# Up projection by seven block products, weight sums in DRAM, out-projection in token halves

## The chip, the cores and the metric

One core of a Trainium2 chip runs the whole kernel. The metric is the device time of one execution in microseconds (us). On this core TensorE (PE) does the matrix products and reads its stationary operand by a weight load of its own (PEld); VectorE (DVE), ScalarE (ACT) and GpSimd (POOL) do the rest, and SyncE (SP) issues all DMAs.

## The reference, cut to what matters

One layer over 16 meta rows and 2048 input rows of width 1024. The kernel cuts the rows into four segments of 512; segment 0 carries the meta rows as well. The part that is changed is the gated MLP and what leads to it.

```python
h = h + mix @ w_out                      # out-projection, 1024 x 1024
z = rmsnorm(h, norm2_g)                  # "z2" in the kernel
u, v = jnp.split(z @ w_up, 2, axis=-1)   # w_up: 1024 x 5632, so D_FF = 2816 = 22 blocks of 128
u = causal_dwconv(u, conv_w, conv_b)     # width 3 along the rows
h = h + (jax.nn.silu(u) * v) @ w_down
```

Everything is float32. The kernel makes each product of two float32 matrices from three passes in the type fp32r: every operand is split into a high part and a low rest, and high x high, high x low and low x high are summed in PSUM. A product over K = 1024 for a 128 x 512 output is therefore 8 x 3 = 24 matmuls.

## The kernel before

`trunk_layer` loops over the four segments `s`. A segment has these stages, in program order: four head pairs of the recurrence (projections f and q, `decays`, `all_scores`, `chunks_out`); the pooling branch; the gates and `mix` (lines 597 to 611); the out-projection (lines 614 to 633); the product `values` for the next segment (lines 647 to 650); and the MLP (lines 654 to 709) in three groups of 8, 8 and 6 units, each followed by its down projection.

`weights()` (line 78) brings one 128 x 1024 block of weights: a DMA of 512 KB into a `raw` buffer (three of them), a cast on ACT for the high part (line 85), a subtraction on DVE for the low part (line 86), both into a `w` buffer (three of them). `proj` (line 101) multiplies such a block with columns of an activation; `rows_product` (line 126) multiplies rows of an activation with weight blocks, over all row chunks for each block, and calls a hook in `between` after each second k.

The out-projection makes h1 for all four chunks of 128 rows, in two halves of the columns (`dh`), 8 weight blocks in all; each block serves 24 matmuls. Between them, as hooks, stand the steps of `norm1(s + 1)`: the first norm of the next segment's rows, transposed and split into `z1`. Then DVE works out the second norm (`inv_rms`), scales the rows (`zt`, line 642), PE transposes them, and ACT and DVE split them into `z2` (`transposed`, line 172). In segments 0 to 2 `to_z2` is a hook inside `values(s + 1)`, which has 96 matmuls on z1; in segment 3 nothing stands beside it. z1 and z2 have buffers of their own.

One unit `j` of the MLP (lines 656 to 678): the u block (24 matmuls over 512 columns; in segment 0 two times 24 over 258 and 256), a copy to SBUF, the convolution on ACT and DVE, a sigmoid; then the v block (24 matmuls over 512 columns), its product with the activated u, and a split into `act`. Two weight blocks a unit.

The order on each engine is made by the framework's scheduler from priorities (program order) and estimated ready times; each engine then runs its own list in that order, and a wait at the head of a list holds what stands behind it. A buffer tag has a fixed number of slots; a new tile waits until a slot's last reader is done.

Of the kernel before, what the change touches and what calls it, by code (L numbers as in the profile page):

```python
# [44 lines left out]
def trunk_layer(ctx: ExitStack, tc: tile.TileContext, x, meta, wts, cst, gf, wpool, out):  # L45
# [6 lines left out]
    xpl = ctx.enter_context(tc.tile_pool(name="xpl", bufs=6))  # L52
# [3 lines left out]
    ps = ctx.enter_context(tc.tile_pool(name="ps", bufs=MM, space=bass.MemoryType.PSUM))  # L56

    V, A, G, T = nc.vector, nc.scalar, nc.gpsimd, nc.tensor

# [3 lines left out]
    for i, (o, n) in enumerate(zip(offs0, sizes0)):  # L63
        t = xpl.tile([P, D], F32, name="xt", tag="xh")
        nc.sync.dma_start(out=t[:n], in_=meta if n < P else x[o - META:o - META + P])
        xt0.append(t)
# [10 lines left out]

    def weights(lo=None):

        i = nxt[0]  # L80
        nxt[0] += 1
        raw = wpl.tile([P, 1024], F32, name="raw", bufs=RAW)
        nc.sync.dma_start(out=raw, in_=wts[i])
        w = wpl.tile([P, 2, 1024], F32R, name="w")
        A.copy(out=w[:, 0, :], in_=raw)  # L85
        (lo or V).tensor_tensor(out=w[:, 1, :], in0=raw, in1=w[:, 0, :].bitcast(F32), op=ALU.subtract)  # L86
        return w
# [38 lines left out]
    def rows_product(src, chunks, nk, consume, between=(), lo=None):  # L126

        banks = [ps.tile([P, 512], F32, name="rp", tag="hg", bufs=HG) if i < HG else
# [43 lines left out]
    def transposed(rows, sizes, offs, dst, gbase):  # L172

        banks = [[i for i in range(len(rows)) if offs[i] + sizes[i] <= 512],
                 [i for i in range(len(rows)) if offs[i] + sizes[i] > 512]]
        for k in range(KB):
            for idx in banks:
                if not idx:
                    continue
# [9 lines left out]
    def norm1_chunk(src, m, off, dst):  # L189
        t = xpl.tile([P, D], F32, name="xt", tag="xh")  # L190
# [19 lines left out]
    def norm1_first(xt, sizes, offs):  # L210

        dst = [blk.tile([P, 2, WMAX], F32R, name="z1") for _ in range(KB)]
# [15 lines left out]
        transposed(xt, sizes, offs, dst, C_G1)  # L228
        return dst

    def norm1(s):
# [3 lines left out]
        def one(c):  # L235
            if c == 0:
                dst.extend(blk.tile([P, 2, WMAX], F32R, name="z1") for _ in range(KB))
# [23 lines left out]
    def decays(f, N):  # L261

        nb = N // BASE
        scr = spl.tile([P, 10, 2 * WMAX // BASE], F32, name="scr", bufs=1)
        tt = spl.tile([P, 2, 2 * WMAX // BASE], F32, name="tt")
        f8 = f.rearrange("p (n j) -> p n j", j=BASE)
        r = [scr[:, i, :nb] for i in range(10)]
# [199 lines left out]
    for i in range(2):  # L467
# [16 lines left out]

    for s in range(nseg):
        nxt[0] = 0
# [9 lines left out]
        for p in range(PAIRS):  # L496
# [18 lines left out]
            main = (m0, NCH, P, W, at[p % 2], bt[p % 2])  # L515
# [98 lines left out]
        sizes2 = ([2] if s == 0 else []) + [P] * NCH  # L614
        offs2 = ([0] if s == 0 else []) + [e0 + c * P for c in range(NCH)]
        h1 = []
        for o, n in zip(offs2, sizes2):
# [3 lines left out]
            else:  # L621
                t = xpl.tile([P, D], F32, name="h1", tag="xh")
                nc.sync.dma_start(out=t, in_=x[s * SEG + o - e0:s * SEG + o - e0 + P])
            h1.append(t)
        chunks, z1n = norm1(s + 1) if s + 1 < nseg else ([], None)
        ss = new_sums(s == 0)
        for dh in range(2):
            def add_h(ci, bank):
                n = sizes2[ci]
                v = h1[ci][:n, dh * 512:(dh + 1) * 512]  # L630
                V.tensor_tensor(out=v, in0=v, in1=bank[:n, :], op=ALU.add)
                square_sums(ss[:n, dh, ci:ci + 1], v, n)
            rows_product(mix, list(zip(offs2, sizes2)), KB, add_h, chunks)


        z2 = [blk.tile([P, 2, WMAX], F32R, name="z2", tag="zo") for _ in range(KB)]
        rs = inv_rms(ss, len(h1))
        rows = []
        for i, n in enumerate(sizes2):
            zt = blk.tile([P, 2, WMAX], F32, name="zt", tag="am")  # L640
            zt = zt.rearrange("p a b -> p (a b)")[:, :D]
            V.tensor_scalar(out=zt[:n], in0=h1[i][:n], scalar1=rs[:n, i:i + 1], scalar2=None, op0=ALU.mult)
            rows.append(zt)
        to_z2 = lambda: transposed(rows, sizes2, offs2, z2, C_G2)


        if s + 1 < nseg:
            z1, vt = z1n, values(s + 1, z1n, between=[to_z2 if i == V_HOOK else (lambda: None) for i in range(V_HOOK + 1)])
        else:
            to_z2()  # L650
        nxt[0] = V_AT + KB // 2


        for (j0, nj) in GROUPS:
            act = [blk.tile([P, 2, WMAX], F32R, name="act", tag="am") for _ in range(nj)]
            for j in range(j0, j0 + nj):
# [124 lines left out]
```

## Time and profile before

| | us |
|---|---|
| median of 3 runs | 3143.08 (3140.93 to 3143.42) |
| the profiled execution, its own time | 3141.98 |
| its span, first to last instruction | 3140.2 |
| PE busy | 3080.5 (98%) |
| DVE busy | 1721.6 (55%) |
| ACT busy | 1136.8 (36%) |
| DMA | 294.86 MB, mean 94 GB/s |
| mean granted TensorE clock | 0.996 |

The profiled execution lies 1.1 us under the median and 1.8 us above its own span. PE's ends are modelled in this profile, so a busy share of a stage says that PE had work without a gap, and the time of one matmul is read from a stretch divided by the matmuls in it.

### The profile page before, as it was taken

To read this page: it belongs to the slowest core of one execution; us is meant where nothing else is said; L and a number is where in the kernel's file an instruction comes from. 1 tells how busy PE (TensorE), PEld (TensorE's weight loads), DVE (VectorE), ACT (ScalarE), POOL (GpSimd) and SP (SyncE) were. 2 spreads that over 40 slices of the span, in tenths; PEclk is the share of its full clock that TensorE was granted. 3 is DMA by queue.
4 is the path that set the end of the run, shared out by engine and by line. 5 is a ranking of instruction groups with operands and counts; after the bars stand their busy time and mean duration, and the time that the engine had idled before them with its cause. 6 is when DMAs were issued, how large, how long until landed. Compare 5 with 4: busy or idle time off the path is not lost.

```text
span 3140.2 us, 45714 instructions
## 1 busy us (share of the span) xinstructions
PE 3080.5 (98%) x19052; PEld 2552.0 (81%) x19052; DVE 1721.6 (55%) x2944; ACT 1136.8 (36%) x1765; POOL 48.9 (2%) x181
## 2 busy tenths in 40 slices
PE   7999999999999999999999999999999999999998
PEld 6899978898877788888877778888887778878887
DVE  5775364454487536544457744554456773354545
ACT  4333244232343325423333433433333432242323
POOL 1000000000000000000000000000000000000000
PEclk9999999999999999999999999999999999999999
DMA  4212232332331223223342133332333122223322
GB/s 153 62 62 81 88 108 88 94 95 93 99 125 62 88 94 114 94 94 94 95 153 69 55 99 105 100 98 94 94 101 128 55 81 94 94 81 94 94 94 88
DMA packets 81747, 294.86 MB, mean 94 GB/s; under 512 B 9074, under 2 KB 9202, under 8 KB 81540
## 3 DMA queue, kind: packets, MB, share of 16 engines
q1 hardware_dynamic: 81540, 291.95, 29.0%
q8 instruction: 149, 2.44, 0.3%
q14 instruction: 58, 0.48, 0.0%
HBM read 283.52 MB, written 8.39 MB: 93 GB/s over the span
## 4 chain that ended last, share of the span: by engine, by line
PE 92%; DVE 6%; ACT 1%; issue 0%; DMA 0%; SPq 0%; DVEq 0%; ACTq 0%
PE pt L108 61%; PE rp L137 24%; PE sp L300 1%; PE up L375 1%; DVE q L259 1%; DVE scr L259 1%; PE sp L312 1%; PE tp L185 1%; DVE k L259 1%; DVE q L513 1%; DVE w L86 1%; PE op L389 1%; PE ktp L366 0%; PE op L394 0%; PE pp L527 0%
## 5 line engine op out<-in xcount | busy, mean ns | idle before, releaser
L108 PE MATMUL pt<-z,w 128*128 128x512 f32 (+3 forms) x9552 | 1939.0, 362 | 0.0
L108 PEld LDWEIGHTS pt<-z,w 128*128 128x128 f32 x9552 | 1596.3, 189 | 296.9 <-issue 10.7
L86 DVE TENSOR_TENSOR w<-raw,w 128x1024 fp32r<-128x1024 f32 x500 | 612.3, 1225 | 1073.1 <-ACT w L85 1069.6
L85 ACT CAST w<-raw 128x1024 fp32r<-128x1024 f32 x504 | 528.3, 1048 | 745.8 <-PE rp L137 358.4
L137 PE MATMUL rp<-w,act 128*128 128x512 f32 x2040 | 474.1, 394 | 0.0
L137 PEld LDWEIGHTS rp<-w,act 128*128 128x128 f32 x2040 | 383.8, 188 | 88.5
L137 PE MATMUL rp<-w,mix 128*128 128x512 f32 (+1 forms) x816 | 192.7, 395 | 0.0
L662 ACT COPY ub<-pt 128x512 f32<-128x512 f32 (+1 forms) x110 | 55.3, 503 | 355.0 <-PE pt L108 355.0
L137 PEld LDWEIGHTS rp<-w,mix 128*128 128x128 f32 (+1 forms) x816 | 147.8, 182 | 39.1 <-issue 2.6
L669 DVE SCALAR_TENSOR_TENSOR cv<-ub,cs,cv 128x512 f32<-128x512 f32 x176 | 131.9, 749 | 3.1
L604 ACT ACTIVATE sg<-pt 128x512 f32<-128x512 f32 (+1 forms) x80 | 41.1, 513 | 239.1 <-PE pt L108 239.1
L672 ACT ACTIVATE sg<-cv 128x512 f32<-128x512 f32 x88 | 55.6, 632 | 178.5 <-DVE cv L669 178.5
L137 PE MATMUL rp<-w,z 128*128 128x512 f32 (+1 forms) x408 | 102.2, 402 | 0.0
L108 PE MATMUL pt<-oa,w 128*128 128x512 f32 (+2 forms) x480 | 95.1, 350 | 0.0
L108 PE MATMUL pt<-ob,w 128*128 128x512 f32 (+2 forms) x480 | 95.0, 350 | 0.0
L673 DVE TENSOR_TENSOR cv<-cv,sg 128x512 f32<-128x512 f32 x88 | 61.0, 693 | 61.5 <-ACT sg L672 61.5
L137 PEld LDWEIGHTS rp<-w,z 128*128 128x128 f32 (+1 forms) x408 | 74.0, 184 | 18.3 <-issue 0.4
L108 PEld LDWEIGHTS pt<-oa,w 128*128 128x128 f32 x480 | 77.9, 189 | 12.5
L108 PEld LDWEIGHTS pt<-ob,w 128*128 128x128 f32 x480 | 77.9, 189 | 12.5
L704 DVE TENSOR_TENSOR h<-h,rp 128x512 f32<-128x512 f32 x96 | 66.0, 688 | 29.1 <-PE rp L137 26.8
L609 DVE TENSOR_TENSOR sg<-sg,pt 128x512 f32<-128x512 f32 (+1 forms) x80 | 46.5, 582 | 62.7 <-PE pt L108 62.6
L95 ACT ACTIVATE z<-tp,cs 128x128 fp32r<-128x128 f32 (+3 forms) x152 | 61.0, 438 | 29.9 <-PE tp L185 12.8
(161 smaller groups left out, 1900.9 us busy)
## 6 DMA issues: line engine op xcount, KB each, us to landing
raw<-in_wts_dram SPq DMA_DIRECT2D x504, 512.0 KB, 3.6
xt<-in_x_dram SPq DMA_DIRECT2D x16, 512.0 KB, 4.5
h<-in_x_dram SPq DMA_DIRECT2D x16, 512.0 KB, 4.6
out_dram<-h SPq DMA_DIRECT2D x12, 512.0 KB, 3.0
gfb<-in_gf_dram SPq DMA_DIRECT2D x8, 256.0 KB, 4.3
out_dram<-h SPq DMA_DIRECT2D x8, 256.0 KB, 2.0
wp<-in_wpool_dram SPq DMA_DIRECT2D x1, 256.0 KB
cs<-in_cst_dram SPq DMA_DIRECT2D x1, 68.0 KB, 5.8
```

The source lines that it names most:

```text
L85: A.copy(out=w[:, 0, :], in_=raw)
L86: (lo or V).tensor_tensor(out=w[:, 1, :], in0=raw, in1=w[:, 0, :].bitcast(F32), op=ALU.subtract)
L95: A.activation(out=dst[0], in_=src, func=AF.Copy, scale=scale)
L108: T.matmul(pt[:, :n], lhsT=w[:, wi, (kof + k) * P:(kof + k + 1) * P], rhs=src[k][:, xi, c0 + o:c0 + o + n], start=(k == 0 and i == 0), sto ...
L137: T.matmul(banks[ci][:n, :], lhsT=src[k][:, xi, o:o + n], rhs=w[:, wi, (k % 2) * 512:(k % 2 + 1) * 512], start=(k == 0 and i == 0), stop=( ...
L259: mul = lambda o, a, b: V.tensor_tensor(out=o, in0=a, in1=b, op=ALU.mult)
L609: V.tensor_tensor(out=gates[i][:, o:o + n], in0=gates[i][:, o:o + n], in1=pt[:, :n], op=ALU.mult)
L662: A.copy(out=ub[:, 2 - e0 + o:2 - e0 + o + n], in_=pt[:, :n])
L669: V.scalar_tensor_tensor(out=cv, in0=ub[:, t_:t_ + SEG], scalar=col(C_CW + t_ * NF, j), in1=cv, op0=ALU.mult, op1=ALU.add)
L672: A.activation(out=sg, in_=cv, func=AF.Sigmoid)
L673: V.tensor_tensor(out=cv, in0=cv, in1=sg, op=ALU.mult)
L704: V.tensor_tensor(out=v, in0=v, in1=bank, op=ALU.add)
```

## The change

In segments 1 to 3 a unit's two blocks of the up projection are taken as one product: the activation side is two halves of the rows (256 columns each) by two halves of K (512 each), the weight side the four 512-deep blocks A11, A12 (u) and A21, A22 (v). A seven-product scheme replaces the eight block products. Each of the seven is 4 x 3 = 12 matmuls over 256 columns (`seventh`). Partial results in the PSUM banks X and Y are copied out by ACT four times a unit and put together by two DVE additions.

- The sums of weights (S1 to S4) are made on DVE in segment 0 (`weight_sums`, four additions of 512 columns a unit) and written to DRAM, `s_d`, with the split A11 and A12, `a_d`: four DMAs of 512 KB a unit. Segments 1 to 3 read per unit two `a_d` halves without splitting, two `s_d` blocks that are split again, and half a block of `wts` (A22). In units 0 to 2 A11 and A12 come from `wts` and are split.
- The activation side has seven slots: two direct quarters, a third quarter, four sums. `to_z2` makes them, once for the first half of the rows, once for the second.
- z1 and z2 share one tag of buffers (`z_plain`, four slots). `norm1(s + 1)` moves from the out-projection into the last down projection of the segment, and `values(s)` to the start of segment s.
- The out-projection runs once for each half of the rows, so that each weight block is brought twice (16 blocks a segment), and a block serves 12 matmuls.
- x and h rows get two tags (four and two slots), the recurrence's `scr` is taken from the second of them, and `at` and `bt` have one buffer instead of two.

The core of the diff:

```diff
+    def seventh(dst, w, xslot, start):
+        for kp in range(KP):
+            for i, (wi, xi) in enumerate(PASS):
+                T.matmul(dst, lhsT=w[:, wi, kp * P:(kp + 1) * P], rhs=z2[kp][:, xi, xslot],
+                         start=(start and kp == 0 and i == 0), stop=(kp == KP - 1 and i == 2),
+                         skip_group_check=True)
+    def q_open(j, iu):
+        if j < OPEN:
+            w = split_weights(wts[iu])[0]
+            a11, a12 = w[:, :, :512], w[:, :, 512:]
+        else:
+            a11, a12 = (blk.tile([P, 2, WMAX], F32R, name="wa", tag="zo")[:, :, :512] for _ in range(2))
+            for i, a in enumerate((a11, a12)):
+                nc.sync.dma_start(out=a.bitcast(F32), in_=a_d[j][i])
...
+        seventh(X[:, HT:], a11, 0, True)
+        seventh(Y[:, :HT], a12, 1, True)
+        A.copy(out=sx[:, :HT], in_=X[:, HT:])
+    def q_rest(j, ig, X, Y, sx, a):
+        w = split_weights(s_d[j][0])[0]
+        seventh(X[:, HT:], w[:, :, :512], 5, False)
+        seventh(Y[:, HT:], w[:, :, 512:], 3, True)
+        A.copy(out=sx[:, HT:], in_=X[:, HT:])
+        w = split_weights(s_d[j][1])[0]
+        seventh(X[:, HT:], w[:, :, :512], 4, False)
+        sy = vpl.tile([P, 512], F32, name="sy", tag="vt")
+        A.copy(out=sy[:, HT:], in_=Y[:, HT:])
+        seventh(Y[:, HT:], w[:, :, 512:], 2, False)
+        A.copy(out=sy[:, :HT], in_=X[:, HT:])
+        ub = new_ub(j)
+        V.tensor_tensor(out=ub[:, 2:2 + SEG], in0=Y, in1=sx, op=ALU.add)
...
+        w = split_weights(wts[ig, :, 512:], 512)[0]
+        seventh(X[:, :HT], w[:, :, :512], 6, True)
+        V.tensor_tensor(out=sy, in0=X, in1=sy, op=ALU.add)
+        gated(cv, sy, a)
+    def weight_sums(j, ru, rg, w):
+        a11, a12, a21, a22 = ru[:, :512], ru[:, 512:], rg[:, :512], rg[:, 512:]
...
+        V.tensor_tensor(out=s1, in0=a21, in1=a22, op=ALU.add)
+        V.tensor_tensor(out=s3, in0=a21, in1=a11, op=ALU.subtract)
+        V.tensor_tensor(out=s2, in0=s1, in1=a11, op=ALU.subtract)
+        V.tensor_tensor(out=s4, in0=a12, in1=s2, op=ALU.subtract)
+        for i in range(2):
+            nc.sync.dma_start(out=s_d[j][i], in_=t[i])
+            nc.sync.dma_start(out=a_d[j][i], in_=w[:, :, i * 512:(i + 1) * 512].bitcast(F32))
```

In `to_z2(half)` of segments 1 to 3, for each of four `kp`, behind four transposes:

```diff
+                for u in range(2):
+                    A.activation(out=a[:, 2 * u + half], in_=tp[:, u * HT:(u + 1) * HT], func=AF.Copy,
+                                 scale=col(C_G2, kp + u * KP))
+                if not half:
+                    split((z[:, 0, 0:2], z[:, 1, 0:2]), a[:, 0:3:2])
+                    continue
+                V.tensor_tensor(out=b[:, 0:2], in0=a[:, 1:2].broadcast_to([P, 2, HT]), in1=a[:, 0:4:3], op=ALU.subtract)
+                V.tensor_tensor(out=b[:, 2], in0=a[:, 3], in1=b[:, 0], op=ALU.subtract)
+                V.tensor_tensor(out=b[:, 3], in0=a[:, 2], in1=b[:, 2], op=ALU.subtract)
+                split((z[:, 0, 3:7], z[:, 1, 3:7]), b)
+                split((z[:, 0, 2], z[:, 1, 2]), a[:, 3])
```

The order in the first group of segments 1 to 3 (`OPEN` is 3):

```diff
+                    if j == 0:
+                        for i in range(OPEN):
+                            opened[i] = q_open(i, at_u(i))
+                            if i == OPEN - 2:
+                                to_z2(1)
+                    if j >= OPEN:
+                        opened[j] = q_open(j, at_u(j))
+                    q_rest(j, at_u(j) + 1, *opened.pop(j), act[j - j0])
```

A unit j of segment 0:

```diff
+                    cv = conv(j, ub)
+                    wg, rg = split_weights(wts[at_u(j) + 1])
+                    part(pg, 0, wg, e0, SEG)
+                    gated(cv, pg, act[j - j0])
+                    weight_sums(j, ru, rg, w)
```

## Rows read from the trace of the kernel before

**Rows 1.** Page, part 1: busy us, share of the span, instructions.

```profile
PE 3080.5 (98%) x19052; PEld 2552.0 (81%) x19052; DVE 1721.6 (55%) x2944; ACT 1136.8 (36%) x1765; POOL 48.9 (2%) x181
```

**Rows 2.** Page, part 4: the chain that ended last, by engine.

```profile
PE 92%; DVE 6%; ACT 1%; issue 0%; DMA 0%; SPq 0%; DVEq 0%; ACTq 0%
```

**Rows 3.** Windows: length, PE, PEld, DVE, ACT, POOL busy; clock, DMA share, GB/s.

```profile
1226.00:1255.50 29.50, 29.50 (x145) 24.25 (x144) 17.89 (x33) 13.59 (x24) 0.00 (x0) 1.00 0.30 90
...
2751.20:2763.70 12.50, 6.84 (x33) 6.29 (x34) 10.35 (x25) 6.52 (x13) 0.00 (x0) 0.73 0.15 43
```

**Rows 4.** Windows of line L108 alone: length, PE busy (matmuls), PEld, clock, DMA.

```profile
258.93:397.74 138.81, 138.81 (x1152) 138.60 (x1152) 1.00 0.30 92
...
1047.87:1181.19 133.32, 133.32 (x576) 108.01 (x576) 1.00 0.30 95
1255.46:1344.22 88.76, 88.76 (x384) 71.76 (x383) 1.00 0.30 94
```

**Rows 5.** Groups by form, PE: count, busy us, mean ns of one.

```profile
L108 PE MATMUL pt<-z,w 128*128 128x512 f32 x6576 | 1568.3, 396 | 0.0
...
L108 PE MATMUL pt<-z,w 128*128 128x256 f32 x1008 | 129.5, 284 | 0.0
```

**Rows 6.** Groups by form, ACT.

```profile
L85 ACT CAST w<-raw 128x1024 fp32r<-128x1024 f32 x504 | 528.3, 1048 | 745.8 <-PE rp L137 358.4 <-PE pt L108 273.4 <-DVE h L704 72.5
...
L92 ACT CAST act<-cv 128x512 fp32r<-128x512 f32 x88 | 54.5, 619 | 0.2 <-DVE cv L676 0.2
L662 ACT COPY ub<-pt 128x512 f32<-128x512 f32 x66 | 38.9, 589 | 268.9 <-PE pt L108 268.9
...
L662 ACT COPY ub<-pt 128x256 f32<-128x256 f32 x22 | 8.2, 372 | 54.4 <-PE pt L108 54.4
...
L95 ACT ACTIVATE ob<-pp,cs 128x256 fp32r<-128x256 f32 x4 | 1.9, 474 | 0.0
```

**Rows 7.** Groups by form, DVE.

```profile
L86 DVE TENSOR_TENSOR w<-raw,w 128x1024 fp32r<-128x1024 f32 x500 | 612.3, 1225 | 1073.1 <-ACT w L85 1069.6
...
L93 DVE TENSOR_TENSOR act<-cv,act 128x512 fp32r<-128x512 f32 x88 | 60.2, 685 | 0.0
...
L259 DVE TENSOR_TENSOR q<-q,tt 128x256 f32<-128x256 f32 x24 | 10.1, 423 | 2.0 <-PE sp L312 1.3
```

**Rows 8.** Windows of all engines in five stages, columns as in rows 3.

```profile
1181.20:1225.60 44.40, 44.40 (x208) 36.09 (x208) 30.06 (x89) 25.36 (x61) 0.00 (x0) 1.00 0.41 131
1255.46:1344.22 88.76, 88.76 (x386) 72.10 (x385) 45.33 (x54) 35.64 (x48) 2.44 (x16) 1.00 0.30 94
1588.46:1621.78 33.32, 33.32 (x146) 27.09 (x145) 13.61 (x16) 10.73 (x19) 0.00 (x0) 1.00 0.34 113
2.00:10.00 8.00, 0.00 (x0) 0.00 (x0) 4.81 (x21) 4.89 (x11) 1.68 (x4) 1.00 0.98 365
484.69:576.41 91.72, 91.72 (x578) 82.84 (x577) 45.52 (x54) 36.94 (x57) 1.48 (x8) 1.00 0.30 93
```

**Rows 9.** Timeline (start, us, instruction): transposes in segment 1; segment 3's gap.

```profile
1240.45 1.91 PE L185 MATMUL tp<-ident,zt 128*128 128x128 f32 x16
...
2749.14 2.77 DVE L631 TENSOR_TENSOR h<-h,rp 128x512 f32<-128x512 f32 x4 [1.15 <-PE rp L137]
...
2756.86 6.80 PE L185 MATMUL tp<-ident,zt 128*128 128x128 f32 x32 [5.67 <-DVE zt L642]
```

**Rows 10.** Windows in and after that gap, columns as in rows 3.

```profile
2757.00:2760.00 3.00, 3.00 (x14) 2.43 (x15) 1.71 (x4) 0.73 (x2) 0.00 (x0) 0.50 0.00 0
...
2763.40:2767.00 3.60, 3.60 (x19) 2.94 (x18) 1.99 (x3) 1.12 (x2) 0.00 (x0) 1.00 0.00 0
```

**Rows 11.** Timeline of one unit's end in segment 1, DVE.

```profile
1267.69 1.23 DVE L86 TENSOR_TENSOR w<-raw,w 128x1024 fp32r<-128x1024 f32 x1 [0.20 <-ACT w L85]
1268.83 0.69 DVE L93 TENSOR_TENSOR act<-cv,act 128x512 fp32r<-128x512 f32 x1
```

**Rows 12.** Page, part 6: DMA issues, KB each, us to landing.

```profile
raw<-in_wts_dram SPq DMA_DIRECT2D x504, 512.0 KB, 3.6
```

More of the change, by code (lines that the diff above doesn't have):

```diff
@@ L81, in weights @@
         nxt[0] += 1
[L82 to L87, printed above, removed]
+        return split_weights(wts[i], lo=lo)[0]
     def split(dst, src, scale=None):
@@ L236, in one @@
             if c == 0:
-                dst.extend(blk.tile([P, 2, WMAX], F32R, name="z1") for _ in range(KB))
+                dst.extend(z_plain())
             if later:
@@ L466, in trunk_layer @@
     at, bt = [], []
-    for i in range(2):
+    for i in range(1):
         a_ = const.tile([P, 2, NCH, P], F32, name=f"at{i}")
@@ L482, in trunk_layer @@
     V.memset(halo, 0.0)
+    s_d = [dram.tile([2, P, 1024], F32, name=f"s_d{j}") for j in range(NF)]
+    a_d = [dram.tile([2, P, 2, 512], F32, name=f"a_d{j}") for j in range(NF)]
     for s in range(nseg):
+        if s > 0:
+            nxt[0] = V_AT
+            vt = values(s, z1)
         nxt[0] = 0
@@ L621, in trunk_layer @@
             else:
-                t = xpl.tile([P, D], F32, name="h1", tag="xh")
+                t = h_row()
                 nc.sync.dma_start(out=t, in_=x[s * SEG + o - e0:s * SEG + o - e0 + P])
             h1.append(t)
[L625 to L633, printed above, removed]
@@ L636, in trunk_layer @@
[L636 to L644, printed above, removed]
@@ new lines, in gated, with part, new_ub @@
+        def gated(cv, g, a):
+            V.tensor_tensor(out=cv, in0=cv, in1=g, op=ALU.mult)
+            split((a[:, 0, :SEG], a[:, 1, :SEG]), cv)
+        def part(pt, po, w, c0, n):
+            for k in range(KB):
+                for i, (wi, xi) in enumerate(PASS):
+                    T.matmul(pt[:, po:po + n], lhsT=w[:, wi, k * P:(k + 1) * P], rhs=z2[k][:, xi, c0:c0 + n],
+                             start=(k == 0 and i == 0), stop=(k == KB - 1 and i == 2))
+        def new_ub(j):
+            ub = tpl.tile([P, TW], F32, name="ub", tag="t")
+            if s > 0:
+                G.tensor_copy(out=ub[:, 0:2], in_=carry[:, j, :])
+            return ub
@@ L708, in add_d @@
                         finish(ci, 1)
-                (rows_one_by_one if end and dh == 1 else rows_product)(act, [(c * P, P) for c in range(NCH)], nj, add_d)
+                rows = [(c * P, P) for c in range(NCH)]
+                if end and dh == 1:
+                    rows_one_by_one(act, rows, nj, add_d)
+                else:
+                    rows_product(act, rows, nj, add_d, chunks)
+            if last and not end:
+                while chunks:
+                    chunks.pop(0)()
+                z1 = z1n
         if s < nseg - 1:
```

194 lines of the change are left out of this document (144 added, 50 removed).

## The prediction

> **What bounds the kernel now.** I read the page's busy shares first: PE is busy 98% of the span, DVE 55% [rows 1]. The chain that ended last says the same by another way: 92% of it is PE, 6% DVE [rows 2]. So a stage costs what its matmuls cost, except where a stretch shows PE idle. The windows by stage show where that is: after the out-projection of segments 1 and 2 PE is busy all 29.50 us, in segment 3 only 6.84 of 12.50 [rows 3]. The windows of the projection line give the price of a matmul. Segments 1 to 3 use 512 columns: 133.32 us / 576 = 231.5 ns and 88.76 / 384 = 231.1 ns. Segment 0 uses 258 and 256 columns: 138.81 / 1152 = 120.5 ns [rows 4]. The groups by form give longer means (396 and 284 ns) [rows 5]; they overlap in the pipeline and are no spacing. DMA moves 94 GB/s at a share of 0.30 in the MLP and reached 365 GB/s in the first microseconds [rows 8].
>
> **What is removed.** A unit of the MLP in segments 1 to 3 takes 48 matmuls of 512 columns, 88.76 / 8 = 11.10 us [rows 4]. It becomes 7 x 12 = 84 matmuls over 256 columns. The nearest row is that of segment 0, with the same weight load: 84 x 120.5 ns = 10.12 us. That is 0.97 us a unit, and for 3 x 22 = 66 units 64.2 us. Four sevenths is the break-even ratio: the change pays only while a 256-column matmul takes less than 11.10 / 84 = 132 ns.
>
> The Trainium skill has a figure that speaks against this: "TensorE: Matmul & The Clock Gate", section "Back-to-back issue gap", gives 81 ns at 128 columns and 131 ns at 512 for sustained streams with their weight loads. My estimate from that page is 98 ns at 256, so 84 x 98 = 8.2 us against 48 x 131 = 6.3 us, a loss of 1.9 us a unit, 127 us in all. The trace does not agree: it shows 231 and 120.5 ns, nearly a halving.
>
> **Does the unit stay PE-bound?** DVE spends 45.33 / 8 = 5.67 us a unit and ACT 35.64 / 8 = 4.46 [rows 8]. DVE gets three more operations of 512 columns (low part of A22, two combining additions), 3 x 0.685 [rows 7], together 7.7 us of 10.1. ACT loses one copy of 0.589 and gains a 512-column cast of 0.619 and four copies of 0.372 [rows 6], 6.0 us. DMA brings 4.5 blocks of 0.524 MB, 2.36 MB in 10.12 us = 233 GB/s, under the 365 seen. So no engine takes over. What is new is a wait inside the unit: each of the four copies must be over before PE may write the bank again, and PE has one product beside it, 12 x 0.1205 = 1.45 us. A copy by itself takes 0.37; behind a weight cast it takes 1.05 + 0.37 = 1.42 [rows 6] plus the hand-overs, which I put at 0.2, and PE loses 0.17 us. Ends: nothing, and all four late, 0.7 us a unit, 46 us. I take 0.1 us a unit, 6.6 us, since ACT is free 4 of 10 us.
>
> **The second norm.** The out-projection's last half ends in a chain: adds, squares, norm, row scaling, transposes. In segment 3 it kept PE idle for 5.67 us, and then paced 32 transposes over 6.55 us, to 2763.41 [rows 9]; in segments 1 and 2 the product `values` hid it [rows 3]. That cover goes to the start of the next segment. In its place stand two openings, 2 x 24 x 0.1205 = 5.8 us. The chain with two row chunks takes about 6 us by the same rows, so the transposes begin nearly in time. Then DVE makes the seven slots. For each of four kp: one operation of 512 columns (0.685), two of 256 (0.423), a low part of 1024 (1.225) and one of 256 (0.423) [rows 7], 3.18 us, 12.7 in all; ACT needs 2 x 0.474 + 1.048 + 0.372 = 2.4 us a kp [rows 6], less than DVE. The first DVE operation starts about 7.5 us after the last matmul, one weight subtraction comes between, and the last low part is there at 21 us. PE has from 6 to 21 the transposes (16, about 1.8 by the stretch in segment 1 [rows 9]), the third opening (2.9) and the products of the first three kp (18 x 0.1205 = 2.2): 8 us idle. In segment 3 the clock fell to its lower level, 1.2 of 2.4 GHz, after such a gap (0.50 granted, 1.00 again 6 us later) [rows 10]; I add 1.5 us for that. So 9.5 us a segment, of which segments 1 and 2 pay 9 each, and segment 3, which had 12.2 us with 3.5 us of PE work for 32 transposes in it, 0.8. In segment 0 the split is the old one and 5.8 us of products lie before it: 1. Together 19.8; ends 5 (other work found for PE) and 35 (DVE also late with weights).
>
> Then units 0 to 2 run without their openings, 60 matmuls in 7.2 us against DVE's 7.7: with the queue left by the slots, 1.5 us a segment, 4.5.
>
> **The first norm moves** into the last down projection. In the out-projection DVE was busy 30.06 of 44.40 us with it; less 8 weight subtractions (9.8), four adds (2.8) and the last mix (2.1) the norm is 15.4 us. The last down projection has 33.32 us with DVE at 13.61 [rows 8], so 29 of 33: it fits with little slack, and x rows now have two slots. I take 1.5 us at each of three seams, 4.5; ends 0 and 15.
>
> **The out-projection** keeps its matmuls, but a block serves 12 x 0.231 = 2.77 us. A raw slot turns over in 3.6 (landing) [rows 12] + 1.05 + 1.23 = 5.9 us, so three slots bring a block each 2.0 us: covered. In segment 0 the two meta rows hold one, for a while two, raw slots: 3 us there; ends 0 and 8.
>
> **Segment 0's sums.** DVE gets 4 x 0.685 = 2.7 us a unit on top of 45.52 / 8 = 5.7 [rows 8], 8.4 of 11.46; DMA moves six blocks, 274 GB/s, under 365. Both fit. Raw blocks u and v are now held until the sums are made, so when the sums run decides when the next v can be loaded. The trace shows engine lists that are not in program order: the next unit's weight subtraction ran before the low part of `act` [rows 11]. So I expect the sums to run in DVE's free time, and take 5 us for the first units, where the queue fills. Ends 0 and 65 (below).
>
> The single `at`/`bt`, the new place of `scr` and the move of `values` itself change no product, and I cost them at nothing: they lie beside projections in stages where PE has work.
>
> **The sum.** -64.2 + 6.6 + 19.8 + 4.5 + 4.5 + 3 + 5 = -20.8 us. Against the profiled execution 3141.98 that is 3121.2; the median lies 1.1 us above it, so 3122 us. About 0.2% (6 us) is what a measurement of this kernel tells from no change.
>
> **The rivals.**
> 1. The seams are hidden: the openings and the partial products cover the slots to 5 us, and the small waits come to 9 instead of 24 us. -64.2 + 5 + 9 = -50, 3093 us. For it: in the MLP of before PE showed no gap at all [rows 3, 8]. Against: DVE's 12.7 us.
> 2. Copies late: ACT's list puts casts ahead of the copies, 0.7 us a unit. -20.8 + 40 = +19, 3162 us. It decides from 0.42 us a unit.
> 3. Slower by the sums: if DVE's list has them behind the gated product, the next v load starts after it. Gated product and low part 1.4, two sums 1.4, issue 0.3, landing 3.6, cast 1.05, low part 1.23, 9.0 us, while PE has 5.9 us of the next u: 3.1 us for 21 units, 65 us. -20.8 - 5 + 65 = +39, 3182 us. It decides from about 1.2 us a unit. For it: program order. Against: rows 11.
> 4. The change doesn't do what it says: the spacing doesn't halve. If it scaled like the mean times, 284 / 396 = 0.72 [rows 5], a matmul would take 166 ns, a unit 13.9 us, and the kernel about 3370 us. The skill's ratio in "TensorE: Matmul & The Clock Gate" would do the like. Against: 120.5 ns over 1152 matmuls.
>
> **How the numbers follow.** Forecast 0.50 (0.47 of it beyond 0.2%), hidden seams 0.17, late copies 0.12 (0.02 faster, 0.04 the same), sums 0.18, spacing 0.03. Faster 0.66, same 0.07, slower 0.27. The low end is 3088, a little under rival 1. The high end is 3170: it takes in late copies and a partial form of the sums, and leaves out the full sums and the spacing. The forecast's own range is 3105 to 3137.
>
> **What would show it.** Spacing: 81 to 82 us for the first group's 8 x 84 matmuls once they run without gaps, against 88.76. Copies: PE idle in the groups of segments 1 to 3, released by ACT. Slots: PE idle of about 8 us in segments 1 to 3 behind the out-projection, ended by DVE on z. Sums: segment 0's first group, 91.72 us before, longer by under 10 us in my case, by 25 in rival 3. Seams: PE idle under 2 us where `values` starts. I am wrong if DVE or a DMA appears on the chain through whole groups.

## The result, and the profile after

The changed kernel takes 3101.66 us (median; 3100.64 to 3108.86), against 3143.25 of the kernel before beside it: ratio 0.9871, 95% interval 0.9852 to 0.9889. It is 41.6 us faster. The forecast was 3122 us, so the gain came out twice as large as the 20.8 us worked out. The profiled execution's span went from 3140.2 to 3100.2 us, 40.0 less; the sums below are made against that.

The page of the changed kernel, busy time by engine (part 1) and the chain that ended last (part 4), answers to [rows 1] and [rows 2]:

```profile
PE 3024.3 (98%) x21452; PEld 2628.2 (85%) x21452; DVE 1971.4 (64%) x3366; ACT 1296.0 (42%) x2130; POOL 65.4 (2%) x180
...
PE 87%; DVE 9%; ACT 2%; DMA 1%; issue 1%; SPq 0%; DVEq 0%; ACTq 0%
```

PE is still what the kernel costs. It has 2400 more matmuls and 56 us less busy time. DVE's share of the chain rose from 6 to 9%, and a DMA has 1%: short stretches are now ended by others. The rest of this section finds them.

Windows (length, PE, PEld, DVE, ACT, POOL busy, granted clock, DMA share, GB/s) of three stages. The first is the second group of segment 1, eight units; the second is the first norm's seam, the last down projection of segment 1; the third is a group of segment 0, where the weight sums are made. They answer to [rows 8]:

```profile
1375.83:1455.86 80.03, 80.03 (x673) 80.03 (x673) 57.78 (x76) 46.22 (x78) 2.47 (x16) 1.00 0.68 229
...
1560.32:1593.50 33.18, 33.10 (x160) 27.07 (x160) 28.11 (x81) 22.25 (x55) 0.99 (x1) 1.00 0.47 159
607.74:699.29 91.55, 91.55 (x577) 82.74 (x577) 63.49 (x83) 36.40 (x55) 1.49 (x8) 1.00 0.69 253
```

Eight units take 80.03 us where they took 88.76 [rows 8], 10.00 us each, and PE is busy through all of it. 80.03 / (8 x 84) = 119.1 ns a matmul. The last down projection takes the first norm in and PE idles 0.08 us. The group of segment 0 takes 91.55 us against 91.72 [rows 8], with 18 us more of DVE and 253 instead of 93 GB/s: in the steady state the sums cost nothing.

**The seam behind the out-projection.** Windows of segment 1, same columns. The out-projection's last matmul ends near 1240.4:

```profile
1239.00:1262.00 23.00, 18.88 (x140) 17.12 (x138) 20.77 (x41) 15.19 (x28) 0.00 (x0) 0.97 0.72 241
1258.00:1262.00 4.00, 1.98 (x9) 1.27 (x9) 3.40 (x5) 1.05 (x1) 0.00 (x0) 0.85 1.01 372
1262.00:1266.00 4.00, 3.96 (x17) 3.67 (x18) 1.23 (x1) 1.69 (x3) 0.00 (x0) 0.50 0.94 346
1266.00:1270.00 4.00, 4.00 (x29) 4.00 (x29) 1.29 (x2) 2.05 (x4) 0.31 (x2) 0.80 0.47 160
1270.00:1275.00 5.00, 5.00 (x44) 5.00 (x43) 4.87 (x8) 3.38 (x8) 0.00 (x0) 1.00 0.45 148
```

What PE waited for in segment 1 from 1194 to 1620 us (total us, times, longest):

```profile
PE X L760 <- ACT z L108: 1.9, 2, 1.2
PE X L760 <- DVE z L109: 1.3, 2, 0.8
PE tp L670 <- DVE xt L700: 0.9, 2, 0.6
```

And the timeline of PE there (start, us, instruction, idle before and what ended it):

```profile
1246.86 0.33 PE L670 MATMUL tp<-ident,xt 128*128 128x128 f32 x1 [0.59 <-DVE xt L700]
...
1252.09 1.34 PE L760 MATMUL X<-z,wa 128*128 128x256 f32 x10
...
1257.96 0.39 PE L760 MATMUL X<-z,w 128*128 128x256 f32 x1 [1.17 <-ACT z L108]
...
1259.29 0.50 PE L760 MATMUL X<-z,w 128*128 128x256 f32 x2 [0.82 <-DVE z L109]
...
1263.22 2.93 PE L760 MATMUL X<-z,w 128*128 128x256 f32 x12
...
1272.44 1.60 PE L760 MATMUL X<-z,w 128*128 128x256 f32 x12
```

The reader sees the seam twice. First as idle time: 4.12 of the 23 us (23.00 - 18.88), half of it in the four microseconds from 1258, where each kp's slots arrive one by one behind DVE's list. Then as clock: after that sparse stretch the granted clock is 0.50, and twelve matmuls take 2.93 us at 1263.22, twelve of the same form 1.60 at 1272.44. A granted clock of 0.85, 0.50 and 0.80 over four microseconds each, between the levels 1.2 and 2.4 GHz, is 1.2 + 4.0 + 1.6 = 6.8 us at the lower one, and half of that, 3.4 us, is work not done. From 1240.4 to the end of the first group at 1331.38 are 91.0 us; less eight units (80.0) and 16 transposes (1.7) that leaves 9.3 us lost in segment 1. 4.2 us of idle time and 3.4 of clock account for most of it. For 1 us of the other 1.7 I have an estimate: a matmul alone is recorded with 0.28 us and the spacing is 0.12, so each of the six waits begins some 0.16 us before PE counts as idle. The rest has no row. Segments 2 and 3 have 91.0 and 91.2 us by the same marks.

**Segment 0.** From the out-projection's start to the first group's end, 396.57 to 563.19, 166.62 us; before 397.74 to 576.41, 178.67, of which `values` (22.2) and the first norm's transposes (3.5) have moved away. So 13.65 us more. What PE waited for from 396 to 872 us:

```profile
PE tp L203 <- DVE ztm L700: 4.7, 1, 4.7
PE tp L203 <- DVE z L112: 3.4, 1, 3.4
```

The two places in the timeline, all engines, and the windows at the two waits (columns as above):

```profile
417.47 1.05 ACT L95 CAST w<-raw 128x1024 fp32r<-128x1024 f32 x1 [1.87 <-issue]
...
434.55 0.56 PE L203 MATMUL tp<-ident,ztm 2*128 2x2 f32 x5 [4.68 <-DVE ztm L700]
...
437.48 1.05 ACT L95 CAST w<-raw 128x1024 fp32r<-128x1024 f32 x1
...
470.89 0.69 DVE L748 TENSOR_TENSOR ws<-raw 128x512 f32<-128x512 f32 x1 [1.69 <-DMA raw<-in_wts_dram]
...
473.43 2.25 DVE L112 SCALAR_TENSOR_TENSOR z<-tp,cs,z 128x256 fp32r<-128x256 f32 x5
473.96 0.69 PE L203 MATMUL tp<-ident,xt 128*128 128x128 f32 x2 [3.42 <-DVE z L112]
```

```profile
434.60:442.00 7.40, 7.29 (x30) 5.57 (x31) 5.93 (x10) 4.94 (x10) 0.00 (x0) 0.54 0.36 122
470.00:482.00 12.00, 8.57 (x52) 8.23 (x51) 8.69 (x16) 3.47 (x9) 0.00 (x0) 0.72 0.88 330
```

At 434.55 PE has nothing but transposes, the meta rows' first: ACT casts no weight block between 417.47 and 437.48. At 470.89 DVE stands at a weight sum whose block has not landed, and five low parts of `z` are behind it in its list, four of which could have run from 471.2 at the latest, when ACT had their high parts done; PE waits 3.42 us for the first of them. Each wait costs twice: behind it the granted clock is 0.54 over 7.4 us and 0.72 over 12 us, up to 3.4 us each of work not done. In the kernel before PE was busy for all of the 178.67 us, at a clock of 1.00.

### The profile page after: what moved, and what is told of

Its sections match the earlier page's. It is cut to its first block, busy times and chain, and to the rows that moved or that the text cites. A ratio compares the mean times of both kernels' runs of the same rounds, so it can differ in the third digit from the quotient of the medians.

```text
span 3100.2 us, 51997 instructions
## 1 busy us (share of the span) xinstructions
PE 3024.3 (98%) x21452; PEld 2628.2 (85%) x21452; DVE 1971.4 (64%) x3366; ACT 1296.0 (42%) x2130; POOL 65.4 (2%) x180
## 3 DMA queue, kind: packets, MB, share of 16 engines
q1 hardware_dynamic: 146260, 436.67, 41.6%
## 4 chain that ended last, share of the span: by engine, by line
PE 87%; DVE 9%; ACT 2%; DMA 1%; issue 1%; SPq 0%; DVEq 0%; ACTq 0%
PE pt L124 30%; PE rp L153 23%; PE X L760 12%; PE Y L760 9%; PE pt L727 8%; PE sp L319 1%; DVE w L96 1%; PE up L394 1%; DVE q L277 1%; PE sp L331 1%; DVE k L277 1%; DVE xt L277 1%; DMA raw<-in_wts_dram 1%; DVE tt L277 1%; DVE q L537 1%
## 5 line engine op out<-in xcount | busy, mean ns | idle before, releaser
L96 DVE TENSOR_TENSOR w<-raw,w 128x1024 fp32r<-128x1024 f32 (+1 forms) x607 | 706.4, 1165 | 751.9 <-ACT w L95 749.8
L124 PE MATMUL pt<-z,w 128*128 128x512 f32 (+3 forms) x4800 | 952.3, 354 | 0.0
L95 ACT CAST w<-raw 128x1024 fp32r<-128x1024 f32 (+1 forms) x611 | 611.1, 1001 | 739.3 <-PE rp L153 281.7
L124 PEld LDWEIGHTS pt<-z,w 128*128 128x128 f32 x4800 | 772.6, 189 | 136.2 <-issue 10.8
L760 PE MATMUL X<-z,w 128*128 128x256 f32 x2484 | 339.3, 286 | 8.7 <-ACT z L108 4.4
L760 PEld LDWEIGHTS X<-z,w 128*128 128x128 f32 x2484 | 316.8, 194 | 12.5 <-DVE z L109 6.1
L727 PE MATMUL pt<-z,w 128*128 128x256 f32 (+2 forms) x1608 | 255.5, 321 | 0.0
L727 PEld LDWEIGHTS pt<-z,w 128*128 128x128 f32 x1608 | 230.9, 191 | 23.2
L760 PE MATMUL Y<-z,w 128*128 128x256 f32 x1692 | 233.4, 286 | 0.0
L760 PEld LDWEIGHTS Y<-z,w 128*128 128x128 f32 x1692 | 218.2, 194 | 0.3
L153 PEld LDWEIGHTS rp<-w,mix 128*128 128x128 f32 (+1 forms) x816 | 148.6, 183 | 40.2 <-issue 4.4
L760 PE MATMUL X<-z,wa 128*128 128x256 f32 x684 | 90.8, 281 | 0.0
```

The lines of the kernel that those rows point to most:

```text
L95: A.copy(out=w[:, 0, :n], in_=raw[:, :n])
L96: (lo or V).tensor_tensor(out=w[:, 1, :n], in0=raw[:, :n], in1=w[:, 0, :n].bitcast(F32), op=ALU.subtract)
L124: T.matmul(pt[:, :n], lhsT=w[:, wi, (kof + k) * P:(kof + k + 1) * P], rhs=src[k][:, xi, c0 + o:c0 + o + n], start=(k == 0 and i == 0), sto ...
L153: T.matmul(banks[ci][:n, :], lhsT=src[k][:, xi, o:o + n], rhs=w[:, wi, (k % 2) * 512:(k % 2 + 1) * 512], start=(k == 0 and i == 0), stop=( ...
L727: T.matmul(pt[:, po:po + n], lhsT=w[:, wi, k * P:(k + 1) * P], rhs=z2[k][:, xi, c0:c0 + n], start=(k == 0 and i == 0), stop=(k == KB - 1 a ...
L760: T.matmul(dst, lhsT=w[:, wi, kp * P:(kp + 1) * P], rhs=z2[kp][:, xi, xslot], start=(start and kp == 0 and i == 0), stop=(kp == KP - 1 and ...
```

## The experiments

Nine kernels, each the changed kernel with one edit, the last with three, and the changed kernel again. Times are medians; the changed kernel's is 3101.7 us. The kernel before, run beside them, took 3143.3 us (products, three operations left out, halves, copies), 3140.7 (order, GpSimd, the two of segment 0) and 3142.9 (all three), so differences of a few us are told by the traces.

### Is it the products? Eight for seven, all moves kept

```diff
-                    q_rest(j, at_u(j) + 1, *opened.pop(j), act[j - j0])
...
+                        w = split_weights(wts[at_u(j)])[0]
+                        ub = new_ub(j)
...
+                        part(pt, 0, w, 0, SEG)
...
-                    weight_sums(0, wu[0][1], rg, wu[0][0])
```

> The changed kernel with everything moved as it is moved (out-projection in row halves, z1 and z2 in one tag, first norm in the last down projection, values at the segment's start), but with the eight block products of before in segments 1 to 3 and without the weight sums. Theory: the gain is the products alone, 66 x (11.10 - 10.00) = 72 us of PE time, and the moves only cost. Then this one loses the 72 us and gets back what the seven slots and the sums cost at the seams (about 13 + 4 us): 3157 us, between 3145 and 3165, slower than the kernel before, with 88.8 us for eight units. Rival: a good part of the gain comes from the moves (first norm and values away from the out-projection): then 3125 us or less.

Measured: 3147.66 us (3146.37 to 3151.95), ratio 1.0021 (1.0012 to 1.0030). The moves of `values`, of the first norm, of the buffers and the token halves cost 4 us together (4 to 9 by the interval), less than the 14 expected, and together bring nothing; the 4.7 us wait for `ztm` is still in this trace. The whole gain is the products': 46 us net of their slots and sums. The rival falls.

### Are the slots the second norm's seam? Three of its operations left out

```diff
-                b = blk.tile([P, 2 * WMAX], F32, name="tb", tag="am")[:, :4 * HT].rearrange("p (u t) -> p u t", t=HT)
-                V.tensor_tensor(out=b[:, 0:2], in0=a[:, 1:2].broadcast_to([P, 2, HT]), in1=a[:, 0:4:3], op=ALU.subtract)
-                V.tensor_tensor(out=b[:, 2], in0=a[:, 3], in1=b[:, 0], op=ALU.subtract)
-                V.tensor_tensor(out=b[:, 3], in0=a[:, 2], in1=b[:, 2], op=ALU.subtract)
-                split((z[:, 0, 3:7], z[:, 1, 3:7]), b)
+                split((z[:, 0, 3:7], z[:, 1, 3:7]), a)
```

> The changed kernel without the three DVE operations that form the activation sums: slots 3 to 6 get the quarters themselves, so that part of the computation is left out. The DVE chain behind the out-projection is 4 x 1.53 = 6.1 us shorter in segments 1 to 3, the products and waits are the same. Theory: the seam (9.3 us lost a segment in the changed kernel, of it some 4 us idle and the rest a lower clock behind it) is bound by DVE: 5 us less a segment, 3086 us, 3082 to 3092, and no drop of the clock. Rival: the seam is set by the weight blocks' landing or by ACT: 3097 us or more, and the clock drops as before.

Measured: 3086.32 us (3083.87 to 3089.60), ratio 0.9828 (0.9812 to 0.9844), 15.3 us under the changed kernel, 5.1 a segment. The trace has no wait of a product for `z` any more, and the granted clock stays at 1.00 from 1239 to 1275 us. What PE still waits for at these seams (whole run), besides 0.7 us for a copy of X:

```profile
PE tp L670 <- DVE xt L696: 2.7, 6, 0.8
```

So the DVE chain bounds the seam, as the theory said. 1.5 us of DVE work a kp (0.685 + 2 x 0.423 [rows 7]), 6.1 a segment, was worth 5.1.

### The same work in another order

The operations of all four kp stay; those that the next product needs first come first.

```diff
-                V.tensor_tensor(out=b[:, 3], in0=a[:, 2], in1=b[:, 2], op=ALU.subtract)
-                split((z[:, 0, 3:7], z[:, 1, 3:7]), b)
-                split((z[:, 0, 2], z[:, 1, 2]), a[:, 3])
+                split((z[:, 0, 3:6], z[:, 1, 3:6]), b[:, 0:3])
+                rest.append((z, a, b))
+            for z, a, b in rest:
+                split((z[:, 0, 2], z[:, 1, 2]), a[:, 3])
+            for z, a, b in rest:
+                V.tensor_tensor(out=b[:, 3], in0=a[:, 2], in1=b[:, 2], op=ALU.subtract)
+                split((z[:, 0, 6], z[:, 1, 6]), b[:, 3])
```

> The changed kernel with the seven slots made in the order in which the products take them: for all four kp first slots 3 to 5 (two operations for the sums, one low part of 768), then slot 2, then slot 6. The DVE work up to the first products' last operand falls from 4 x 3.18 to about 4 x 2.1 us. Theory (the seam is bound by DVE's chain): 3.5 to 5 us less a segment with the lower clock's share, 3089 us (3085 to 3094). Rival: the later slots are then the wait, and nothing or little is won: 3099 us or more.

Measured: 3092.82 us (3088.49 to 3093.59), ratio 0.9844 (0.9829 to 0.9858), 8.8 us under the changed kernel. In segments 1 to 3 its waits for `z` are gone, and a smaller one for the weight cast has come up (whole run):

```profile
PE X L765 <- ACT w L95: 2.5, 3, 1.0
```

### The same work on another engine: low parts of three and a half weight blocks on GpSimd

```diff
-                w = split_weights(wts[iu])[0]
+                w = split_weights(wts[iu], lo=G if j == OPEN - 1 else None)[0]
...
-            w = split_weights(s_d[j][0])[0]
+            w = split_weights(s_d[j][0], lo=G if j == 0 else None)[0]
...
```

> The changed kernel with the low parts of the third opening's and unit 0's weight blocks on GpSimd in segments 1 to 3 (2.58 us each there instead of 1.23 on DVE). DVE's list in the seam loses 2.45 us. Theory: 2 us less a segment, 3096 us (3092 to 3099). Rival: GpSimd's low parts come too late for the products, or slow DVE beside them: 3102 us or more.

Measured: 3120.45 us (3119.09 to 3124.98), ratio 0.9937 (0.9922 to 0.9952): 19 us slower than the changed kernel. The theory fell; the rival's second form, that they slow DVE, held. The wait that grew is on DVE, in a step that the edit does not touch: PE waits 18.3 us, six times, for the row scaling `xt`, 4.3 us in the changed kernel. The wait (whole run), and the timeline of that kernel, DVE and POOL, in segments 1 and 3:

```profile
PE tp L670 <- DVE xt L700: 18.3, 6, 6.2
...
1239.59 2.41 POOL L96 TENSOR_TENSOR w<-raw,w 128x1024 fp32r<-128x1024 f32 x1 [78.63 <-ACT w L95]
...
1240.77 1.24 DVE L177 TENSOR_TENSOR nrm<-ss 128x2 f32<-128x2 f32 x1 [0.90 <-ACT jk L171]
...
1242.04 0.17 DVE L178 TENSOR_SCALAR nrm<-nrm 128x2 f32<-128x2 f32 x1
...
1242.33 4.74 POOL L96 TENSOR_TENSOR w<-raw,w 128x1024 fp32r<-128x1024 f32 x2 [0.34 <-PE X L760]
...
1242.45 2.27 DVE L164 SCALAR_TENSOR_TENSOR nrm<-nrm 128x2 f32<-128x2 f32 x1
...
1244.76 2.33 DVE L165 TENSOR_TENSOR nrm<-nrm 128x2 f32<-128x2 f32 x1
...
1248.50 1.41 DVE L700 TENSOR_SCALAR xt<-h,nrm 128x1024 f32<-128x1024 f32 x2
...
2749.34 7.11 POOL L96 TENSOR_TENSOR w<-raw,w 128x1024 fp32r<-128x1024 f32 x3 [79.11 <-ACT w L95]
...
2751.80 2.38 DVE L178 TENSOR_SCALAR nrm<-nrm 128x2 f32<-128x2 f32 x1
...
2754.21 2.26 DVE L161 TENSOR_SCALAR nrm<-nrm 128x2 int32<-128x2 int32 x1
```

The same steps on DVE in the changed kernel, segment 1:

```profile
1243.69 0.16 DVE L177 TENSOR_TENSOR nrm<-ss 128x2 f32<-128x2 f32 x1
...
1244.29 0.16 DVE L164 SCALAR_TENSOR_TENSOR nrm<-nrm 128x2 f32<-128x2 f32 x1
1244.48 0.16 DVE L165 TENSOR_TENSOR nrm<-nrm 128x2 f32<-128x2 f32 x1
...
1246.05 1.42 DVE L700 TENSOR_SCALAR xt<-h,nrm 128x1024 f32<-128x1024 f32 x2
```

Operations on two columns that take 0.16 us now take 1.24, 2.27 and 2.33, and each ends where an operation of GpSimd ends: 1242.0 against 1239.59 + 2.41 = 1242.00; 1244.7 against half of the 4.74 from 1242.33, 1244.70; 1247.09 against 1247.07. The operation with one input (L178) at 1242.04 keeps its 0.17, but it lies between two operations of GpSimd. In segment 3 three of them run back to back, and there the operations with one input are the ones held: L178 takes 2.38 us and L161 2.26, again until an operation of GpSimd ends (two thirds of the 7.11 us and the whole from 2749.34 are 2754.08 and 2756.45). So two inputs are not the condition here. In segment 1 the three lose 5.35 us together. The row scaling begins 10.9 us after the first product that follows the out-projection (1237.64) instead of 5.7 (1240.37), 5.2 later: the same amount, on the path that PE waits for. PE is idle for 5.77 us in front of the transposes, and the granted clock behind that is 0.52 from 1249 to 1255 us, so this gap too costs more than its length. "SBUF — State Buffer" of the Trainium skill, section "Who interferes with whom", says that a VectorE instruction with two SBUF inputs and a GpSimd instruction that reads SBUF exclude each other for a whole instruction, whichever began first; the rows of segment 1 agree, with GpSimd first each time. The rows of segment 3 show the same wait for operations with one input from SBUF, which that sentence does not cover.

### Token halves in the out-projection undone

```diff
-        for half, idx in enumerate(halves):
-            ss = new_sums(first_s and not half)
-            ... rows_product of the half's rows, twice over the weight blocks
+        for dh in range(2):
+            rows_product(mix, list(zip(offs2, sizes2)), KB, add_h)
+        rs = inv_rms(ss, len(h1))
+        for half, idx in enumerate(halves): row scaling, to_z2(0) behind the first
```

> The changed kernel with the out-projection in one pass over all row chunks, so that each weight block is brought once and the first half of the slots is made behind it too. Theory: the halves pay for themselves by the openings that stand beside the second norm; without them PE has nothing for 5.7 us of the chain and some 4 us of the first slots, then the 8 us wait as before: 8 us more in each of segments 1 to 3, and in segment 0 about nothing, as the raw slots are less pressed there: 3126 us, 3115 to 3140. Rival: the doubled weight blocks cost as much as the halves hide: 3102 us, within 5.

Measured: 3120.86 us (3118.43 to 3124.61), ratio 0.9936 (0.9921 to 0.9950), 19 us slower than the changed kernel, inside the theory's range, so the halves are worth 19 us. The wait is one a segment (whole run):

```profile
PE tp L670 <- DVE xt L699: 17.0, 3, 5.7
```

The halves bring each weight block twice in order to put half of the norm beside matmuls; 5.7 us is the norm's chain of adds, squares and scaling in the open, the 5.67 us of [rows 9] again.

### Do the four copies of a unit cost? Each done twice

```diff
-            A.copy(out=sx[:, :HT], in_=X[:, HT:])
+            for _ in range(2):
+                A.copy(out=sx[:, :HT], in_=X[:, HT:])
...                                                # the same for the other three
```

> The changed kernel with each of the four copies out of PSUM done twice in a row: 1.5 us more of ACT a unit, and each hand-over to PE 0.37 us later. Theory: the copies have slack, since PE has a product of 1.43 us beside each and showed no wait at them: at most 0.1 us a unit, 3102 to 3109 us. Rival: they are near the edge, as the prediction priced them: 0.37 us later is mostly seen, 4 x 0.2 to 4 x 0.37 us a unit, 3155 to 3200 us.

Measured: 3122.25 us (3119.61 to 3126.11), ratio 0.9940 (0.9924 to 0.9956), 20.6 us more, 0.31 us a unit: neither expectation. Three doubled copies show no wait, one does. Timeline of a unit with doubled copies:

```profile
1393.37 0.36 ACT L791 COPY sy<-Y 128x256 f32<-128x256 f32 x1
...
1393.63 1.05 ACT L95 CAST w<-raw 128x1024 fp32r<-128x1024 f32 x1
...
1394.58 0.37 ACT L791 COPY sy<-Y 128x256 f32<-128x256 f32 x1
...
1395.01 1.50 PEld L760 LDWEIGHTS Y<-z,w 128*128 128x128 f32 x12 [0.23 <-ACT sy L791]
```

The second copy is behind a weight cast of 1.05 us, and the next product's first weight load stands 0.23 us for it. With single copies the rows are these, of the changed kernel:

```profile
1389.91 1.60 PE L760 MATMUL Y<-z,w 128*128 128x256 f32 x12
1390.11 0.37 ACT L784 COPY sx<-X 128x256 f32<-128x256 f32 x1 [0.78 <-PE X L760]
...
1391.35 1.60 PE L760 MATMUL X<-z,w 128*128 128x256 f32 x12
...
1391.55 0.38 ACT L788 COPY sy<-Y 128x256 f32<-128x256 f32 x1
...
1392.79 1.60 PE L760 MATMUL Y<-z,w 128*128 128x256 f32 x12
```

A copy ends 0.87 us before PE writes its bank again (1390.48 to 1391.35, 1391.93 to 1392.79). That is room for a second copy, and not for a cast and a copy, 1.42. By the same rows a single copy behind the cast would end at 1391.55 + 1.42 = 1392.97, 0.18 us after 1392.79: an estimate that agrees with the forecast's 0.17. No run has that order; in the changed kernel the cast comes behind the copy.

### Segment 0's two waits, one at a time

The meta rows out of the weight blocks' slots:

```diff
-                t = wpl.tile([P, D], F32, name="h1m", tag="raw", bufs=RAW)
+                t = blk.tile([P, 2 * WMAX], F32, name="h1m", tag="zo")[:, :D]
...                                                # ztm likewise
```

> The changed kernel with the two meta rows of segment 0 (h1m and its scaled copy) in the tag of the pooling branch's buffers instead of the weight blocks' raw slots. In the changed kernel PE waits 4.7 us for the scaled meta rows and then goes through the transposes with nothing between them, 434.5 to 439.7 us, and ACT shows no weight cast between 418.5 and 437.5. Theory: the two held raw slots starve the out-projection's second half of weight blocks; with free slots those products stand before and between the transposes: 6 us less, 3096 us (3092 to 3099). Rival: the transposes stand that early because of the hook's place and estimate, and PE waits all the same: 3100 us or more.

Measured: 3096.49 us (3092.61 to 3097.01), ratio 0.9854 (0.9838 to 0.9871), 5.2 us less than the changed kernel, and the wait for `ztm` is gone.

The first weight sums behind the last low part of `z` in DVE's list:

```diff
-                    weight_sums(0, wu[0][1], rg, wu[0][0])
+                    with tc.issue_after(z_low.ins):
+                        weight_sums(0, wu[0][1], rg, wu[0][0])
```

> The changed kernel with one order edge on DVE: the weight sums of segment 0 are issued behind the last low part of the second norm. In the changed kernel DVE waits 1.7 us for a raw block with the four sums of unit 0 at the head of its list, runs them for 2.5 us, and the low parts of z2 stand behind them; PE waits 3.4 us for these. Theory: 4 us less, 3098 us (3095 to 3100). Rival: later sums hold the raw blocks of unit 0 longer and the wait moves to unit 1's second block: 3102 to 3108.

Measured: 3096.94 us (3095.61 to 3099.87), ratio 0.9861 (0.9846 to 0.9876), 4.7 us less, and the wait for `z` of L112 is gone. The interval of each ratio is as wide as the gain, about 5 us either way; it is the wait that disappears from the trace that says which it was. The stretch that both edits touch, from the out-projection's start to the first group's end in segment 0, says it more sharply than the medians: 166.6 us in the changed kernel (164.2 to 167.4 in the traces whose edits leave it alone), 159.7 with the meta rows moved, 159.8 with the sums behind `z`.

### All three, and the changed kernel beside it

The edits of the slots' order, of the meta rows and of the sums' place in one kernel:

> Three edits to the changed kernel at once: h1m and ztm in a tag of their own, the weight sums of the first opening behind the last low part of z, and the slots made in the order in which the seventh product needs them. Theory: each takes away a wait at another place (segment 0's out-projection, segment 0's first opening, the three second openings), so the gains that were measured for each alone (5.2, 4.7 and 8.8 us) add up: 3083 us (3079 to 3089). Rival: two of them free the same time, since the first two both lie between segment 0's first norm and its first group; then 3088 us or more.

> The changed kernel itself, beside the kernel with the three edits on the same chip: 3101 us (3098 to 3105) by its own runs; the difference between the two is the worth of the three edits.

Measured: 3078.84 us (3075.09 to 3080.51), ratio 0.9803 (0.9789 to 0.9816), against 3103.49 (3101.47 to 3103.86), ratio 0.9878 (0.9864 to 0.9891). The three are worth 24.7 us together, where the gains one by one make 18.7, and the time lies just under the theory's range; the gap is within their intervals, and the rival, that two of them free the same time, falls. Read from the stretches that the edits touch, out-projection's start to the first group's end, the gains do add up: 6.9 and 6.8 us in segment 0 and 12.1 in segments 1 to 3 for the slots, 25.8 in all, against 26.6 in the kernel with all three. Part of that is clock: the mean granted clock of the profiled run is 0.997 against 0.991, at most 0.6% of the span, 19 us. It is the fastest kernel of the study, 64 us under the kernel before. Its windows at the seam of segment 1, same columns as above; its out-projection there ends 11.5 us earlier than in the changed kernel, so 1246.5 us answers to 1258:

```profile
1246.50:1250.50 4.00, 3.77 (x32) 3.62 (x31) 3.76 (x11) 3.49 (x9) 0.00 (x0) 1.00 0.85 271
1250.50:1254.50 4.00, 4.00 (x35) 3.89 (x33) 3.95 (x6) 2.25 (x5) 1.17 (x2) 1.00 0.86 299
1254.50:1258.50 4.00, 3.64 (x27) 3.22 (x26) 2.42 (x4) 1.83 (x4) 0.00 (x0) 1.00 1.04 409
```

With the gaps nearly closed the clock stays at 1.00: the stretch that lost 3.4 us to it loses nothing.

## Why the prediction was right or wrong

The sign and the mechanism held: the gain is the spacing of the matmuls, less what the slots and sums cost at the seams, and PE still bounds the kernel. The size was half. By the terms of the sum, from spans and windows:

| term | predicted us | measured us | read from |
|---|---|---|---|
| products, 66 units | -64.2 | -72.0 | 66 x (88.76 - 80.03) / 8 |
| copies in the unit | +6.6 | 0 | PE and PEld busy 80.03 of 80.03 |
| second norm, segments 1 to 3 | +18.8 | +17.0 | out-projection's start to the first group's end: 137.0, 136.9 and 137.2 us for 137.3, 137.3 and 145.8 (without `values` and the first norm), and 8.73 for eight units given back in each |
| units 0 to 2 without openings | +4.5 | 0 | no wait of PE there but those for slots |
| first norm's seams | +4.5 | +1.2 | 0.4 at each |
| segment 0 (second norm 1, raw slots 3, sums 5) | +9 | +13.65 | 166.62 us for 152.97 |
| sum | -20.8 | -40.2 | span -40.0 |

**The products** were mis-sized by 1.4 ns a matmul. The row of 120.5 ns mixed matmuls of 258 and 256 columns [rows 4]; 256 alone, in segments 1 to 3, take 119.1. A column more on the mean is 231.1 / 512 = 0.45 ns, so the mixture explains a third of it. Most of the rest lies in the starts of the matmuls in the group from 1375.83: those on the stored halves `wa` follow each other after 117.1 ns on the mean, those on `w`, the tile that segment 0 uses, after 119.9. Two products of seven are on `wa`, 0.8 ns on the mean of all. Why `wa` is quicker no run shows. That small step is 84 x 66 x 1.4 ns = 7.8 us, the largest of the misses: where a term is a count of thousands, the last nanosecond of its price carries as much as a whole seam.

The estimate of 98 ns from "TensorE: Matmul & The Clock Gate" in the Trainium skill, with 131 ns at 512 columns, would have made the kernel slower. The trace of the changed kernel decides as the one before did: 119.1 ns, and 231 at 512 [rows 4].

**The copies** were the step that failed. I charged 0.1 us a unit for copies that queue behind a cast; the timeline has the casts behind the copies, and each copy 0.87 us of room. The doubled copies show that PE can be made to wait in this way (0.31 us a unit when a cast stands between a copy and its double). Rival 2, all four copies late, did not occur, and its price of 0.7 us a unit was not measured.

**The second norm** came out at the predicted size, 9.3 us a segment for 9.5, with other parts: 4.2 us idle, 3.4 of clock and 1.7 without a wait of their own, where I had 8 and 1.5. PE had a product there that I had not given it, 24 matmuls of unit 3's opening with the stored halves A11 and A12 (the `X<-z,wa` at 1252.09 is part of it), 2.9 us of work where I had idle time; and the sparse stretch after it cost more clock than the closed gap of [rows 10] had suggested. That DVE's slots are the cause is shown twice, by leaving out work (-15.3 us) and by its order alone (-8.8 us). Rival 1's hidden seam is possible, though this kernel did not have it: with three edits, one of them the order of the slots, the clock stays up and the time is 3079 us, under rival 1's 3093.

**Units 0 to 2** cost nothing: the forecast let DVE's queue run on, 1.5 us a segment, but PE's waits end with the slots. Why DVE had caught up by then I have not followed further.

**The first norm** fitted into the down projection at 0.4 us a seam, not 1.5. DVE is busy 28.11 of 33.18 us there, near the 29 that I had added up; a full engine whose result is not yet wanted costs nothing.

**Segment 0** was too cheap. The two waits and the clock behind them carry nearly all of the 13.65 us. By the stretch, the raw slots took 6.9 us (166.6 to 159.7; predicted 3, upper end 8) and the sums 6.8 (to 159.8; predicted 5); by the medians 5.2 and 4.7. With both edits and the slots' order the stretch is 154.1, 1.1 over the 152.97 of before, which is what the forecast gave the second norm there. Over the idle time shown, 4.7 and 3.4 us, that is 2.2 and 3.4 more, which the lower clock behind each wait accounts for; the forecast had such a term in segments 1 to 3 and none here. The sums did not cost what I had named, a queue that fills over the first units. It was rival 3 once instead of 21 times: a sum that stood in DVE's list ahead of work that was ready, 3.42 us and the clock behind it. In the steady group rival 3 has no place: 91.55 us for 91.72.

**What was right by chance.** The second norm's size came out right from parts that were wrong. The forecast's own range, 3105 to 3137, did not hold the time; the range given, 3088 to 3170, did, because it reached to rival 1, whose time was nearly met by another way (dearer seams, cheaper products and copies).

## What to carry to other kernels

Seven products for eight pay when PE is busy and the price of a matmul follows its columns: read that price from windows of one line over hundreds of matmuls at exactly the new size, not from the mean of a group, and multiply it out before anything else. Expect the cost at the seams, where the new operands are made: order their making by when the first product needs each, and look for what stands ahead of it in an engine's list with a wait of its own. Count a gap of PE together with the clock behind it: here waits of 4.7 and 3.4 us cost 6.9 and 6.8 in their stretch. Do not move work to GpSimd beside a short dependent chain on DVE without looking at that chain's instructions one by one.

## What the runs showed of the hardware that was not expected

- A subtraction of 128x1024 on GpSimd (2.4 us) held up DVE's operations on two columns until its end: 0.16 us became 1.24, 2.27 and 2.33 us for operations with two inputs in segment 1, and 0.17 became 2.38 and 2.26 for operations with one input in segment 3.
- PE was not idle for long anywhere in segment 1's seam (1.17 us at most), yet after four microseconds with 1.98 us of work the granted clock was 0.50 in the next four, with PE busy 3.96 of them; it was at 1.00 again in the window from 1270 us. Twelve matmuls of 256 columns took 2.93 us at the lower level and 1.60 at the upper.
- 119.1 ns a matmul of 256 columns with a new weight load each, held over 672 matmuls beside DMA at 229 GB/s and a share of 0.68: the transfers, 229 GB/s where there were 94 [rows 8], cost PE nothing that the windows show. By the starts, matmuls whose weights lie in `wa` follow each other after 117.1 ns, those with weights in `w` after 119.9; no run tests why.
